# A decoder layer on one core: the inverse root with its own sign, and two of three block sums on GpSimd

## The chip, the core and the metric

The kernel runs on one core of a Trainium2 chip. A core has a matrix engine (TensorE, PE in the profile), a vector engine (VectorE, DVE), a scalar engine (ScalarE, ACT), a general engine (GpSimd, POOL) and SyncE (SP), which issues transfers. They run side by side and wait for each other on semaphores. Operands lie in SBUF, sums of products in PSUM, which has eight banks here. The metric is the device time of one execution in microseconds; lower is better.

## The reference, cut to what matters

One layer of width 1024 on 1024 positions in float32. Every row is normed, multiplied into nine groups of columns, mixed by two kinds of attention, multiplied back and normed again:

```python
def rms_norm(x, g):
    xf = x.astype(jnp.float32)
    y = xf * lax.rsqrt(jnp.mean(xf * xf, axis=-1, keepdims=True) + NORM_EPS)
    return (y * g.astype(jnp.float32)).astype(x.dtype)

def hybrid_layer(x, layer_idx, pre_g, post_g, w_in, ...):
    h = rms_norm(x, pre_g)
    z = jnp.einsum('bsd,de->bse', h, w_in)
    qa, ka, va, ga, qb, kb, vb, gb, gk_low = split_columns(z)
    oa = diff_attention(...)          # 8 heads, softmax minus lam times a second softmax
    oa = rms_norm(oa, subln_g) * (1.0 - lam_init) * silu(ga)
    ob = gla_chunked(...)             # 4 heads, gated linear attention
    ob = rms_norm(ob, gla_g) * silu(gb)
    y = jnp.einsum('bse,ed->bsd', jnp.concatenate([oa, ob], axis=-1), w_out)
    return x + rms_norm(y, post_g)
```

## The kernel before

**Stages.** First x is loaded in eight tiles of 128 rows, normed, transposed and scaled by pre_g: this gives h with the model's columns on the partitions. Then h is multiplied by w_in, pair of column groups after pair, with the results stored to memory (up to about 630 us). Then the scores and weights of the eight softmax heads are made, while PE also multiplies by w_out. At the end eight tiles of y are summed, normed and added to x.

**Products in two parts.** Each float32 operand is cut into a rounded part (hi, a cast on ScalarE) and the rest (lo, a subtraction on DVE), and three products are made of them. `parts` (L545) does it for a block of h, `make_weights` (L278, lines 315 and 316) for a block of w_in, L1096 and L1097 for the weights of the softmax.

**Seven products for eight.** w_in and h are cut into 2 x 2 blocks, and each pair of column groups is multiplied by Winograd's scheme with seven products, numbered 1 to 7 in `order`; `LEFT` says which block or sum of blocks of h each takes: h11, h12, s4, h22, s1, s2, s3. The sums of h's blocks are made in `blocks(j)` for j = 0 to 3, each one quarter of the columns: s1 = h21 + h22 (L565, from PSUM), s3 = h11 - h21 (L568, written over h21) and s2 = s1 - h11 (L569, written over h11, which lies in the tile f1hi). ScalarE and DVE then cut each into hi and lo (L547, L548). s4 = h12 - s2 follows at L625. In the profile the sums' own names are h, f1hi and s. Between two calls of `blocks` PE makes one of the early products (`go(1)`), so that the sums must be ready from product 5 (the tiles named z, which take s1), product 6 (x, which takes s2) and product 7 (s3) on.

**The inverse root.** `rstd` makes 1/sqrt(s + eps) from Ln and Exp on ScalarE and one step of Newton's method on DVE. As it stands, the step ends with (t - 1.5) * r, so its result has the wrong sign. The callers put that right: `scale_x` multiplies by -1 as its second factor, and at the end GpSimd multiplies post_g by -1 (L1408).

**What sets the order.** PE's instructions, and a few that are named in the code (`pin`, `keep_in_program_order`), stand as written. All others are put in order for each engine by a scheduler that has its own times for instructions; it runs when the program is built. Banks of PSUM go round: `take_bank` takes the one that was freed first, so that an early product waits until DVE or ScalarE has read the transposes that had the bank before. DVE's L565 frees such banks.

Of the kernel before, what the change touches and what calls it, by code (L numbers as in the profile page):

```python
# [11 lines left out]
ALU = mybir.AluOpType  # L12
# [19 lines left out]
def hymba_kernel(  # L32
# [20 lines left out]
    nc = tc.nc  # L53
    act, dve, pool, pe, sp = nc.scalar, nc.vector, nc.gpsimd, nc.tensor, nc.sync
# [55 lines left out]
    def take_bank(shape, name):  # L110
        i = free.pop(0)
        return bank(i, shape, name), i
# [6 lines left out]
    def tr(dst, src):  # L119
        tc.keep_in_program_order(pe.transpose(dst, src, ident))  # L120
# [11 lines left out]
    def block(n):  # L132
        if n not in H:
            pool_h, pieces = (hpool, 1) if n in ("s3", "s4") else (hw, 2)
            H[n] = [
                [
                    pool_h.tile(
                        [P, HB // pieces, 512], F32R, tag=f"{n}_{part}{i}", name=f"{n}_{part}"
                    )
                    for i in range(pieces)  # L140
                ]
                for part in ("hi", "lo")
            ]
        return H[n]
# [15 lines left out]
    def t_c(name, dt=F32):  # L160
        return t2k("c", 4, name, dt)
# [317 lines left out]

    def scale_x(st, cs, engine=pool):  # L480
        x_cs = xs[st][:, cs]
        return engine.tensor_scalar(x_cs, x_cs, norms[st], -1.0, ALU.mult, ALU.mult)

    norms, normed = {}, []

    def norm_x(*sts):
        n = len(sts)
        ssq = const.tile([P, 4, n], F32, tag=f"ssq{sts[0]}", name="ssq", bufs=1)
        for i, st in enumerate(sts):
            junk = hw.tile([P, D], F32, tag=("s2_hi0", "s2_lo0")[st % 2], name="junk")  # L490
            ins = act.activation(
                junk, xs[st], AF.Square, scale=D**-0.5, accum_out=ssq[:, 0, i : i + 1]
            )
            if n == 1:
                tc.keep_in_program_order(ins)
        pin = tc.keep_in_program_order if n == 1 else None
        normed[:] = [rstd(nc, ssq[:, :, :n], ssq[:, 0, :n], eps_t, pin)]
        for i, st in enumerate(sts):
            norms[st] = ssq[:, 1, i : i + 1]
            if n == 1:  # L500
                pin(scale_x(st, cols(0), dve))
            else:
                scale_x(st, slice(0, D))
# [12 lines left out]
    for st in range(4):  # L516
        scale_x(st, cols(1))

    def put(ps, k, dst, j):
        hi, lo = dst  # L520
        act.activation(at(hi, j), ps, AF.Copy, scale=pre_g[:, k : k + 1])
        dve.scalar_tensor_tensor(
            at(lo, j), ps, pre_g[:, k : k + 1], fp(at(hi, j)), ALU.mult, ALU.subtract
        )
# [20 lines left out]
    def parts(n, j, f):  # L545
        hi, lo = block(n)
        act.copy(at(hi, j), f)  # L547
        dve.tensor_tensor(at(lo, j), f, fp(at(hi, j)), ALU.subtract)  # L548

    def blocks(j):  # L550


        pss = []
        for k in (j, j + HB):
            ps, i = take_bank([P, 512], "xT")
            for n in range(4):
                tr(ps[:, n * P : (n + 1) * P], xs[4 + n][:, k * P : (k + 1) * P])
            pss.append(ps)
            free.append(i)
        k = j + HB  # L560
        h21 = t_c("h21")
        act.activation(h21, pss[0], AF.Copy, scale=pre_g[:, j : j + 1])
        put(pss[1], k, block("h22"), j)
        s1 = t_c("s1")
        dve.scalar_tensor_tensor(s1, pss[1], pre_g[:, k : k + 1], h21, ALU.mult, ALU.add)  # L565
        parts("s1", j, s1)
        h11 = f1[0][:, j]
        dve.tensor_tensor(h21, h11, h21, ALU.subtract)  # L568
        dve.tensor_tensor(h11, s1, h11, ALU.subtract)  # L569
        parts("s2", j, h11)  # L570
        parts("s3", j, h21)

# [46 lines left out]
    for j in range(HB):  # L619
        blocks(j)  # L620
        go(1)
# [782 lines left out]
    fin = ctx.enter_context(tc.tile_pool(name="fin", bufs=3, reuse_waits="tile"))  # L1404
    post_g = fin.tile([P, D], F32, name="post_g", bufs=1)
    sp.dma_start(post_g, post_norm_g[0:1, :].to_broadcast([P, D]))

    pool.tensor_scalar(post_g, post_g, -1.0, None, ALU.mult)  # L1408
    banks = [Y[0], Y[1], SC[0], SC[1], SC[2], PO, TR[0], TR[1]]
    raws_d, yps, xts = {}, {}, {}  # L1410

# [25 lines left out]
    def finish(n):  # L1437
# [4 lines left out]
        for dh in range(2):  # L1442
# [6 lines left out]
            if not dh:  # L1449
                dve.tensor_scalar(ssq[:, 0], ssq[:, 2], EPS, None, ALU.add)  # L1450
                if n >= NT - LAST:
                    dve.tensor_tensor(y[:, cols(0)], ps_d[st, 0], post_g[:, cols(0)], ALU.mult)
        ins = rstd(nc, ssq, ssq[:, 3], ssq[:, 0])[2]
        if n >= NT - LAST:
            with tc.issue_after(ins.ins):
# [22 lines left out]
def rstd(nc, t, s, eps, pin=None):  # L1478

    pin = pin or (lambda ins: ins)  # L1480
    pin(nc.scalar.activation(t[:, 1], s, AF.Ln, bias=eps))
    exp = pin(nc.scalar.activation(t[:, 1], t[:, 1], AF.Exp, scale=-0.5))
    half = pin(nc.vector.tensor_scalar(t[:, 2], s, eps, 0.5, ALU.add, ALU.mult))
    if t.shape[2] == 1:
        pin(nc.vector.scalar_tensor_tensor(
            t[:, 2], t[:, 1], t[:, 2], t[:, 1], ALU.mult, ALU.mult
        ))
    else:
        pin(nc.vector.tensor_tensor(t[:, 2], t[:, 2], t[:, 1], ALU.mult))
        pin(nc.vector.tensor_tensor(t[:, 2], t[:, 2], t[:, 1], ALU.mult))  # L1490
    last = nc.vector.scalar_tensor_tensor(
        t[:, 1], t[:, 2], 1.5, t[:, 1], ALU.subtract, ALU.mult
    )
    return exp, pin(last), half

# [31 lines left out]
```

## Time and profile before

| | us |
|---|---|
| three runs | 982.34, 983.35, 983.55 (median 983.35) |
| profiled execution | 981.88 |
| its span, first to last instruction | 980.2 |
| busy: PE, DVE, ACT, POOL | 957.5, 737.7, 600.1, 138.1 |
| granted clock of TensorE | 0.998 of full speed |

In the profile a row of a timeline reads: start in us from the span's start, duration in us, engine, line of the kernel, operation, out<-in by the program's names, and in brackets the idle time before it and what ended it. Rows of equal instructions that follow each other are merged (x4). In a list of waits, the engine and line that waited stand first, then what it waited for, the total, how many times, and the longest. PEld is the loading of PE's stationary operand.

### The profile page before, as it was taken

Reading aid. Unit: us, or ns where it says so; the run is one execution under the profiler, and the core shown is the slowest. Engines: PE = TensorE matmul, PEld = TensorE weight load, DVE = VectorE, ACT = ScalarE, POOL = GpSimd, SP = SyncE. Lnnn points to the kernel's source line nnn. Section 1 sums busy time; section 2 is a strip of 40 time slices with the busy share of each in tenths; the row PEclk is TensorE's granted clock in tenths of the full one; section 3 lists DMA queues with packets and bytes.
Section 4 is the critical chain, followed back from the end, with each engine's and each line's share of the span. In section 5 each row is a group of like instructions: output and inputs, shape, how many; then the busy total and the mean of one; then the engine's idle time right before and its main releaser. Section 6 shows DMA issues by size and latency. Waiting matters only on the chain.

```text
span 980.2 us, 15757 instructions
## 1 busy us (share of the span) xinstructions
PE 957.5 (98%) x5338; PEld 829.9 (85%) x5338; DVE 737.7 (75%) x1452; ACT 600.1 (61%) x1164; POOL 138.1 (14%) x143
## 2 busy tenths in 40 slices
PE   6999999999999999999999999999999999999997
PEld 5998988888889998899888888878888888888785
DVE  6986697798866677585885876587888888898555
ACT  8642365486367455445565765366786777787673
POOL 4300000000000010000200100021322222433422
PEclk9999999999999999999999999999999999999999
DMA  9443456747765868896987866997656669994677
GB/s 353 141 122 93 124 153 196 234 164 236 257 228 169 268 193 266 256 292 222 298 255 236 278 208 224 355 308 249 220 173 229 223 208 355 322 288 110 136 210 145
DMA packets 152593, 220.45 MB, mean 225 GB/s; under 512 B 17104, under 2 KB 83664, under 8 KB 152416
## 3 DMA queue, kind: packets, MB, share of 16 engines
q1 hardware_dynamic: 148480, 212.10, 66.8%
q0 software_dynamic: 4032, 7.34, 4.8%
q8 instruction: 42, 0.69, 0.3%
q14 instruction: 39, 0.32, 0.1%
HBM read 133.93 MB, written 88.60 MB: 227 GB/s over the span
## 4 chain that ended last, share of the span: by engine, by line
PE 75%; DVE 8%; DMA 8%; ACT 3%; issue 3%; SPq 1%; POOL 0%; DVEq 0%; ACTq 0%; POOLq 0%
PE x L117 17%; PE ypart L117 12%; PE y L117 12%; PE z L117 12%; PE sc L117 7%; PE po L117 5%; PE yps L117 4%; PE wtr L120 3%; DMA wo_d<-wo_raw 2%; DVE w L316 1%; PE gpo L117 1%; DMA wo_raw<-in_w_out_dram 1%; DVE w_raw L296 1%; DMA w_raw<-in_w_in_dram 1%; DMA mixd<-gate 1%
## 5 line engine op out<-in xcount | busy, mean ns | idle before, releaser
L315 ACT CAST w<-w_raw 128x512 fp32r<-128x512 f32 (+1 forms) x164 | 112.3, 688 | 94.5 <-PE y L117 44.2
L316 DVE TENSOR_TENSOR w<-w_raw,w 128x512 fp32r<-128x512 f32 (+1 forms) x164 | 126.5, 774 | 49.8 <-ACT w L315 43.5
L1048 ACT ACTIVATE p<-p,stt 128x896 f32<-128x896 f32 (+7 forms) x128 | 99.3, 776 | 36.3 <-DVE stt L1038 34.5
L427 ACT COPY s<-x 128x512 f32<-128x512 f32 x84 | 49.1, 584 | 83.2 <-PE x L117 80.2
L296 DVE TENSOR_TENSOR w_raw<-w_raw 128x512 f32<-128x512 f32 (+1 forms) x96 | 76.7, 799 | 15.9 <-DMA w_raw<-in_w_in_dram 14.6
L1054 POOL TENSOR_SCALAR p<-p,stt,lam 128x1024 f32<-128x1024 f32 (+3 forms) x64 | 56.2, 879 | 226.1 <-DVE stt L1053 226.0
L775 POOL TENSOR_SCALAR_AFFINE_SELECT gan<-gan 128x512 f32<-128x512 f32 x8 | 17.3, 2159 | 488.2 <-ACT gan L774 488.2
L1038 DVE CUSTOM_DVE_ANT_0 p<-sc,maskt 128x512 f32<-128x512 f32 (+3 forms) x128 | 74.4, 585 | 15.2 <-PE sc L117 13.7
L117 PE MATMUL z<-s_hi,w 128*128 128x512 f32 x320 | 79.7, 391 | 0.0
L117 PE MATMUL y<-h_hi,w 128*128 128x512 f32 x320 | 79.6, 391 | 0.0
L117 PE MATMUL x<-s_hi,w 128*128 128x512 f32 x320 | 79.6, 391 | 0.0
L117 PE MATMUL ypart<-wo_hi,m_hi 128*128 128x512 f32 x192 | 79.0, 411 | 0.1
L117 PE MATMUL ypart<-wo_hi,m_lo 128*128 128x512 f32 x192 | 75.5, 393 | 0.0
L117 PE MATMUL ypart<-wo_lo,m_hi 128*128 128x512 f32 x192 | 75.4, 393 | 0.0
L117 PE MATMUL sc<-k,q 128*128 128x512 f32 (+1 forms) x192 | 70.5, 371 | 1.5 <-DVE stt L1038 1.5
L117 PEld LDWEIGHTS x<-s_hi,w 128*128 128x128 f32 x320 | 59.7, 188 | 12.2
L117 PEld LDWEIGHTS y<-h_hi,w 128*128 128x128 f32 x320 | 59.6, 188 | 12.2
L117 PEld LDWEIGHTS z<-s_hi,w 128*128 128x128 f32 x320 | 59.5, 188 | 12.0
L117 PE MATMUL sc<-ks,q 128*128 128x512 f32 (+1 forms) x192 | 66.3, 348 | 0.0
L1096 ACT CAST wt_hi<-wtr 128x512 fp32r<-128x512 f32 (+1 forms) x80 | 42.7, 534 | 24.7 <-PE wtr L120 24.3
L1097 DVE TENSOR_TENSOR wt_lo<-wtr,wt_hi 128x512 fp32r<-128x512 f32 (+1 forms) x80 | 50.7, 633 | 7.8 <-ACT wt_hi L1096 7.2
L1057 DVE SCALAR_TENSOR_TENSOR p<-p,stt,p 128x1024 f32<-128x1024 f32 (+3 forms) x64 | 52.1, 814 | 4.7 <-POOL p L1054 4.4
(225 smaller groups left out, 2241.9 us busy)
## 6 DMA issues: line engine op xcount, KB each, us to landing
w_raw<-in_w_in_dram SPq DMA_DIRECT2D x56, 512.0 KB, 4.7
wo_raw<-in_w_out_dram SPq DMA_DIRECT2D x32, 256.0 KB, 3.1
wo_d<-wo_hi SPq DMA_DIRECT2D x32, 256.0 KB, 3.2
wo_d<-wo_raw SPq DMA_DIRECT2D x32, 256.0 KB, 4.2
q<-q_d SPq DMA_DIRECT2D x32, 256.0 KB, 4.7
k<-k_d SPq DMA_DIRECT2D x32, 256.0 KB, 5.5
ks<-k_d SPq DMA_DIRECT2D x64, 128.0 KB, 6.2
wo_hi<-wo_d SPq DMA_DIRECT2D x16, 512.0 KB, 6.4
```

The lines of the kernel that those rows point to most:

```text
L117: tc.keep_in_program_order(pe.matmul(*a, **k))
L120: tc.keep_in_program_order(pe.transpose(dst, src, ident))
L296: dve.tensor_tensor(dst, a, b, ALU.subtract)
L315: act.copy(w[0], src)
L316: dve.tensor_tensor(w[1], src, fp(w[0]), ALU.subtract)
L427: act.copy(b[k], ps)
L1038: ins = dve.tensor_tensor_reduce(p[:, a:e], sc[:, : e - a], maskt[:, NZ + P - (e - a) :] if last else maskt[:, : e - a], 1.0, 3e38 if i == ...
L1048: act.activation(p[:, :n], p[:, :n], AF.Exp, bias=st[:, m : m + 1], scale=-1.0, accum_out=st[:, 2 + m : 3 + m],)
L1054: pool.tensor_scalar(p1[:, :n], p1[:, :n], st[:, 5:6], lam, ALU.mult, ALU.mult)
L1057: dve.scalar_tensor_tensor(p0[:, :n], p0[:, :n], st[:, 4:5], p1[:, :n], ALU.mult, ALU.subtract)
L1096: act.copy(hi[:, :n], pt[:, :n])
L1097: dve.tensor_tensor(lo[:, :n], pt[:, :n], fp(hi[:, :n]), ALU.subtract)
```

## The change

It does three things. The step in `rstd` ends with the right sign: the half takes the factor -0.5 for 0.5 and the last operation adds for it subtracts. So `scale_x` multiplies by 1.0, and the product on post_g on GpSimd is left out. And the two sums L568 and L569 in `blocks`, four times each, are issued on GpSimd and no more on DVE; s1 stays on DVE, since it reads PSUM.

```diff
     def scale_x(st, cs, engine=pool):
         x_cs = xs[st][:, cs]
-        return engine.tensor_scalar(x_cs, x_cs, norms[st], -1.0, ALU.mult, ALU.mult)
+        return engine.tensor_scalar(x_cs, x_cs, norms[st], 1.0, ALU.mult, ALU.mult)
...
         dve.scalar_tensor_tensor(s1, pss[1], pre_g[:, k : k + 1], h21, ALU.mult, ALU.add)
         parts("s1", j, s1)
         h11 = f1[0][:, j]
-        dve.tensor_tensor(h21, h11, h21, ALU.subtract)
-        dve.tensor_tensor(h11, s1, h11, ALU.subtract)
+        pool.tensor_tensor(h21, h11, h21, ALU.subtract)
+        pool.tensor_tensor(h11, s1, h11, ALU.subtract)
         parts("s2", j, h11)
         parts("s3", j, h21)
...
     sp.dma_start(post_g, post_norm_g[0:1, :].to_broadcast([P, D]))
-
-    pool.tensor_scalar(post_g, post_g, -1.0, None, ALU.mult)
...
-    half = pin(nc.vector.tensor_scalar(t[:, 2], s, eps, 0.5, ALU.add, ALU.mult))
+    half = pin(nc.vector.tensor_scalar(t[:, 2], s, eps, -0.5, ALU.add, ALU.mult))
...
     last = nc.vector.scalar_tensor_tensor(
-        t[:, 1], t[:, 2], 1.5, t[:, 1], ALU.subtract, ALU.mult
+        t[:, 1], t[:, 2], 1.5, t[:, 1], ALU.add, ALU.mult
     )
```

The lines up to L1405 keep their numbers; later ones move up by two. The scheduler puts some other instructions in another order too. On DVE, from the s1 of block 1 to the s1 of block 2 (h21_491 and f1hi are block 0's difference and sum, h21_556 block 1's difference, xT_605 block 2's transposes), there stood:

```order
L565 SCALAR_TENSOR_TENSOR s1_560<-xT_551,pre_g_58,h21_556 128x512
L316 TENSOR_TENSOR w_570<-w_early_218,w_570 128x512
L548 TENSOR_TENSOR s2_lo_511<-f1hi_261,s2_hi_509 128x512
L568 TENSOR_TENSOR h21_556<-f1hi_261,h21_556 128x512
L316 TENSOR_TENSOR w_624<-w_early_218,w_624 128x512
L569 TENSOR_TENSOR f1hi_261<-s1_560,f1hi_261 128x512
L548 TENSOR_TENSOR s1_lo_503<-s1_560,s1_hi_501 128x512
L403 TENSOR_TENSOR gv_st_652<-y_627,s_544 128x512
L522 SCALAR_TENSOR_TENSOR h22_lo_496<-xT_605,pre_g_58,h22_hi_494 128x512
L565 SCALAR_TENSOR_TENSOR s1_614<-xT_605,pre_g_58,h21_610 128x512
```

and now stands:

```order
L565 SCALAR_TENSOR_TENSOR s1_560<-xT_551,pre_g_58,h21_556 128x512
L548 TENSOR_TENSOR s3_lo_516<-h21_491,s3_hi_515 128x512
L316 TENSOR_TENSOR w_570<-w_early_218,w_570 128x512
L548 TENSOR_TENSOR s2_lo_511<-f1hi_261,s2_hi_509 128x512
L316 TENSOR_TENSOR w_624<-w_early_218,w_624 128x512
L548 TENSOR_TENSOR s1_lo_503<-s1_560,s1_hi_501 128x512
L403 TENSOR_TENSOR gv_st_652<-y_627,s_544 128x512
L522 SCALAR_TENSOR_TENSOR h22_lo_496<-xT_605,pre_g_58,h22_hi_494 128x512
L565 SCALAR_TENSOR_TENSOR s1_614<-xT_605,pre_g_58,h21_610 128x512
```

The two sums are gone, and the lo part of block 0's difference, which stood ahead of block 1, stands behind its s1. On GpSimd the sums stand between the memsets of a later stage (gkl, wl2), which wait for DVE's second L316 above and for PE's last transposes:

```order
L639 MEMSET ku_773 128x8
L568 TENSOR_TENSOR h21_491<-f1hi_261,h21_491 128x512
L569 TENSOR_TENSOR f1hi_261<-s1_499,f1hi_261 128x512
L568 TENSOR_TENSOR h21_556<-f1hi_261,h21_556 128x512
L569 TENSOR_TENSOR f1hi_261<-s1_560,f1hi_261 128x512
L651 MEMSET gkl_772 128x1024
L646 MEMSET wl2_963 128x768
L568 TENSOR_TENSOR h21_610<-f1hi_261,h21_610 128x512
L569 TENSOR_TENSOR f1hi_261<-s1_614,f1hi_261 128x512
L568 TENSOR_TENSOR h21_666<-f1hi_261,h21_666 128x512
L569 TENSOR_TENSOR f1hi_261<-s1_670,f1hi_261 128x512
```

The memsets stood there before too, with nothing between them. On DVE, ahead of the second L316 of product 6's weights (w_731, the one on which PE waits in the profile) the end of the queue was, from L296 on:

```order
L296 TENSOR_TENSOR w_raw_198<-w_raw_212,w_raw_198 128x1024
L625 TENSOR_TENSOR s4_757<-f1lo_262,f1hi_261 128x512
L569 TENSOR_TENSOR f1hi_261<-s1_670,f1hi_261 128x512
L548 TENSOR_TENSOR s2_lo_512<-f1hi_261,s2_hi_510 128x512
L440 TENSOR_TENSOR c_747<-y_734,s_727 128x512
L548 TENSOR_TENSOR s3_lo_516<-h21_666,s3_hi_515 128x512
L296 TENSOR_TENSOR w_raw_200<-w_raw_200,w_raw_198 128x1024
L316 TENSOR_TENSOR w_731<-w_raw_198,w_730 128x1024
```

In the change the fourth L625 and the last L548 of s2 come ahead of that L316, which they followed; PE's order is the same in both.

## The prediction

> **What bounds the kernel now.** I read the page first, then who waited for whom on TensorE (PE), then the busy times by stretch, and only then the two places where PE waits for VectorE (DVE). The page says that PE is nearly always busy, and GpSimd (POOL) nearly always idle:
>
> ```profile
> span 980.2 us, 15757 instructions
> PE 957.5 (98%) x5338; PEld 829.9 (85%) x5338; DVE 737.7 (75%) x1452; ACT 600.1 (61%) x1164; POOL 138.1 (14%) x143
> ```
>
> So work taken off DVE is worth something only where PE waits for DVE. The waits of PE (what, total us, times, longest) and the busy times of three stretches (length, then PE, PEld, DVE, ACT, POOL, clock, DMA share, GB/s):
>
> ```profile
> PE xT L120 <- DVE x L482: 8.9, 4, 7.4
> PE po L117 <- DVE wt_lo L1097: 1.7, 1, 1.7
> PE y L117 <- DVE s L565: 1.3, 1, 1.3
> ...
> 41.00:60.00 19.00, 17.57 (x124) 16.20 (x122) 19.00 (x29) 9.96 (x16) 0.74 (x1) 1.00 0.17 48
> ...
> 140.00:480.00 340.00, 339.28 (x1967) 300.16 (x1966) 255.28 (x398) 186.94 (x321) 13.09 (x6) 1.00 0.72 231
> 480.00:920.00 440.00, 438.02 (x2249) 369.77 (x2248) 341.22 (x809) 301.12 (x624) 90.21 (x94) 1.00 0.78 249
> ```
>
> From 41 to 60 us, where the sums of h's blocks are made, DVE is busy for 19.00 of 19.00 us while PE stands still for 1.4 us: PE has almost no cover left there. From 140 to 920 us PE is idle for 0.72 + 1.98 us, so a delay that it takes at 60 us finds next to nothing to absorb it and arrives at the end nearly whole. The clock is 1.00 in all three. The 8.9 us at L482 are the first loads and norms; the change gives them another factor of the same cost and no other order.
>
> **Part 1: eight sums go from DVE to GpSimd.** L568 and L569 run four times each. What DVE is spared is read from this timeline (start, us, engine):
>
> ```profile
> 32.91 1.03 PE L120 MATMUL xT<-ident,xt 128*128 128x128 f32 x8
> ...
> 36.77 0.68 DVE L316 TENSOR_TENSOR w<-w_early,w 128x512 fp32r<-128x512 f32 x1
> ...
> 39.45 1.12 PE L117 MATMUL y<-w,h_lo 128*128 128x256 f32 x8
> ...
> 40.61 0.69 DVE L403 TENSOR_TENSOR gv_st<-y,s 128x512 f32<-128x512 f32 x1
> 41.22 0.74 DVE L522 SCALAR_TENSOR_TENSOR h_lo<-xT,pre_g,h_hi 128x512 fp32r<-128x512 f32 x1
> 41.87 0.74 DVE L565 SCALAR_TENSOR_TENSOR s<-xT,pre_g,h 128x512 f32<-128x512 f32 x1
> 42.76 2.14 PE L117 MATMUL y<-w,h_hi 128*128 128x256 f32 x16 [1.32 <-DVE s L565]
> ...
> 49.19 0.69 DVE L569 TENSOR_TENSOR f1hi<-s,f1hi 128x512 f32<-128x512 f32 x1
> 49.79 0.69 DVE L568 TENSOR_TENSOR h<-f1hi,h 128x512 f32<-128x512 f32 x1
> 50.39 0.69 DVE L548 TENSOR_TENSOR s_lo<-h,s_hi 128x512 fp32r<-128x512 f32 x1
> 51.60 1.22 DVE L296 TENSOR_TENSOR w_raw<-w_raw 128x1024 f32<-128x1024 f32 x1
> 53.08 1.12 PE L117 MATMUL z<-w,s_lo 128*128 128x256 f32 x8
> 56.87 1.22 DVE L316 TENSOR_TENSOR w<-w_raw,w 128x1024 fp32r<-128x1024 f32 x1
> 56.92 2.44 PE L117 MATMUL x<-w,s_hi 128*128 128x256 f32 x16
> ```
>
> Starts of neighbours are 0.60 us apart (49.19, 49.79, 50.39), so each sum moved frees 0.60 us of DVE. Of its other instructions in the walk below, those with 512 columns take 0.60 (L522 and L565 0.65, by 41.22 and 41.87), those with 1024 1.15. What they cost on GpSimd, and what this does to DVE, is shown a little earlier, where GpSimd makes four two-input sums of the same shape (L542) while DVE has other work; the last row is the group of the four (count, then busy us and mean ns):
>
> ```profile
> 18.16 1.28 POOL L542 TENSOR_TENSOR f1hi<-h_hi,h_lo 128x512 f32<-128x512 f32 x1
> 19.41 2.27 POOL L542 TENSOR_TENSOR f1hi<-h_hi,h_lo 128x512 f32<-128x512 f32 x1
> ...
> 18.18 2.34 DVE L296 TENSOR_TENSOR w_raw<-w_raw 128x1024 f32<-128x1024 f32 x1
> 20.45 1.25 DVE L1483 TENSOR_SCALAR ssq<-ssq,eps_t 128x2 f32<-128x2 f32 x1
> 21.69 1.21 DVE L296 TENSOR_TENSOR w_raw<-w_raw 128x1024 f32<-128x1024 f32 x1
> ...
> L542 POOL TENSOR_TENSOR f1hi<-h_hi,h_lo 128x512 f32<-128x512 f32 x4 | 6.0, 1529 | 3.0 <-DVE h_lo L522 3.0
> ```
>
> Read them as turns. The GpSimd sum that starts at 18.16 runs its 1.28 us; the DVE subtraction issued at 18.18 takes 2.34 us instead of 1.21, because it begins when that sum ends (18.16 + 1.28 = 19.44, and 19.44 + 1.1 = 20.5). The next GpSimd sum, 2.27 us instead of 1.28, begins when the DVE instruction ends, and a DVE instruction on two columns waits 1.25 us for it. The two engines take turns, instruction by instruction, and whoever waited longest goes next. DVE instructions that read PSUM are outside of it: during GpSimd's L482, four instructions from 23.93 to 29.34, this one took the usual 0.74 us:
>
> ```profile
> 23.93 5.41 POOL L482 TENSOR_SCALAR xt<-xt,ssq 128x1024 f32<-128x1024 f32 x4 [2.25 <-ACT h_hi L521]
> 25.16 0.74 DVE L522 SCALAR_TENSOR_TENSOR h_lo<-xT,pre_g,h_hi 128x512 fp32r<-128x512 f32 x1
> ```
>
> Of DVE's instructions around the sums, L548, L316, L296 and L625 read two operands from SBUF, so these can be held; L522, L565, L403 and L440 read PSUM. The unknown is for how long each new GpSimd sum holds DVE: at least 0, at most 1.53 us (the mean of the four L542, their own waits included); I take 1.25, the spacing of two starts (18.16 to 19.41).
>
> Now the queue. By the order of the changed program, DVE goes from block 1's L565 to the L316 on which PE waits last (started at 56.87) as follows. I let a GpSimd sum go once its L565 is done and DVE's current instruction has ended. Block 1: s_lo 36.7 to 37.3, GpSimd's L568 to 38.5, L316 to 39.1, L569 to 40.4, s_lo, L316, s_lo to 42.2, then L403, L522, L565 from 43.4. This L565 freed PE's bank from 41.87 before: PE restarts 1.5 us late. Block 2, whose first GpSimd sum follows the two memsets: s_lo to 44.7, L568 to 45.9, L625 to 46.5, L569 to 47.8, L625, s_lo, L522, L565, s_lo to 50.9. Block 3: L568 to 52.1, s_lo to 52.7, L569 to 54.0, L316 to 55.1, L625, L403, three s_lo and one more to 58.1 (PE wants the last s_lo of s1 soon after its 53.08), L296, L625, s_lo, L440, L296 to 62.2. The L316 then starts at 62.2 against 56.87, 5.3 us late, and PE's second third of that x with it.
>
> The same from the other side: in the 20.1 us from 36.77 to 56.87 six of the eight sums leave (6 x 0.60 = 3.6; block 0's two lie ahead of it, where DVE waits for block 1's transposes, which PE starts at 32.91, anyway); by the new order three instructions of 0.60 us come to stand ahead of the L316 (a first s_lo, the last L625 and the last s_lo: +1.8); six holds of 1.25 come in, each of them with an L548, L316 or L625 next on DVE (+7.5). -3.6 + 1.8 + 7.5 = +5.7, less the idle moments that it fills. I take the walk's **+5.3 us**. From there DVE and PE are late together, and no further wait arises: ScalarE has half of its time free in that stretch (9.96 of 19.00). Its casts of s2 and s3 now wait for GpSimd, with bank-freeing L562 and weight cast L315 queued behind them, but in the walk they come ahead of the DVE instruction that uses them.
>
> The GPSIMD Engine Reference of the Trainium skill, section Elementwise — side-by-side cycle accounting, measures 4497 ns for such a sum on 2048 columns; a quarter is, as an estimate, 1.12 us. By that the sum would be 6 x 0.13 us smaller, +4.5; the row with the duration decides.
>
> **Part 2: the product on post_g goes (L1408).** Here are the last DVE wait of PE and what lies around it:
>
> ```profile
> 925.56 2.69 DVE L1348 TENSOR_TENSOR m_lo<-m_raw,m_hi 128x384 fp32r<-128x384 f32 x2
> 925.99 3.12 POOL L1408 TENSOR_SCALAR post_g<-post_g 128x1024 f32<-128x1024 f32 x1
> 926.36 0.62 ACT L1129 CAST sq_hl<-sq 64x512 fp32r<-64x512 f32 x1
> 927.41 0.50 PE L117 MATMUL po<-wt_hi,v 128*128 128x256 f32 x2
> 928.28 0.69 DVE L1130 TENSOR_TENSOR sq_hl<-sq,sq_hl 64x512 fp32r<-64x512 f32 x1
> 929.00 0.56 DVE L1097 TENSOR_TENSOR wt_lo<-wtr,wt_hi 128x384 fp32r<-128x384 f32 x1
> 929.61 0.39 PE L117 MATMUL po<-wt_lo,v 128*128 128x256 f32 x1 [1.70 <-DVE wt_lo L1097]
> ...
> 946.79 0.56 DVE L1232 TENSOR_TENSOR m_lo<-m_raw,m_hi 128x384 fp32r<-128x384 f32 x1
> ```
>
> Two DVE instructions take 2.69 us; one of that shape takes 0.56 (946.79). Without the hold they end near 926.7; L1130 waits for ACT until 926.98 and ends at 927.6; L1097 starts at 927.62 instead of 929.00. That is **-1.4 us**, with bounds of 0 (L1408 is not what holds) and -1.7 (PE's whole wait). The chain that ended last shows why it arrives whole; from 930.56 on it is PE alone (with one ms product between):
>
> ```profile
> 930.56 8.41 PE yps L117 x37
> ...
> 939.20 34.28 PE yps L117 x151
> ```
>
>  That ScalarE's order in the last tiles changes (the seeds of tile 4 ahead of an Exp) costs nothing: some five instructions of 0.6 us now stand ahead of tile 4's operands, while PE spends 24 matmuls of 34.28 / 151 = 0.23 us, 5.4 us, on the tile before.
>
> **Other edits.** The signs in rstd and scale_x are other constants in the same instructions: 0. In the first scores one L1057 moves ahead of a 0.48 us score instruction; PE waits earlier but for the same next bank: 0, at most 0.5 either way.
>
> Sum: +5.3 - 1.4 = **+3.9 us**. The profiled execution took 981.88 us with a span of 980.2, 1.5 under the median of 983.35; a span of 984.1 is expected and, added to the median, 987.2 us.
>
> **Rivals.** (a) *No turns*: these forms run side by side, as the undisturbed 1.28 of the sum at 18.16 might suggest. Then DVE is free early; but L403 still waits for PE's y, which ends at 40.57 (39.45 + 1.12), L565 still starts near 41.8, and only the wait for L316 (0.3 us: the x of 16 takes 2.44, the y of the same shape 2.14) and 0.3 more are won: -0.6 - 1.4 = -2.0, 981.3. Against it: 2.34 beside 1.21. (b) *DVE keeps its turn*: a DVE instruction that stands ready goes before GpSimd's, whose sums start only where DVE idles or reads PSUM. Then some 0.6 us of each hold lies under such an instruction: 5.3 - 6 x 0.6 - 1.4 = +0.3, 983.7. Against it: at 20.45 DVE had an instruction ready, and GpSimd went. The SBUF — State Buffer page of the Trainium skill, section Who interferes with whom, has it that issue order decides who is blocked, not the kind of instruction; this would come out as (b) where DVE always issues first. (c) *L1408 did not hold DVE*, since a descriptor-writing L1313 stands right before it: no gain in part 2, +5.3, 988.6. (d) *Longer holds*, 1.53 each: 1.7 more, 988.9.
>
> **How the numbers follow.** Forecast 0.60 (986 to 988.3), (a) 0.12, (b) 0.13, (c) 0.08, (d) 0.07. About 0.2%, 2 us, is what a measurement here can tell from no change. Slower by more: forecast, (c), (d), less some 0.05 of the forecast that falls short: 0.70. Within: (b) and that rest, 0.17. Faster: (a) at its edge, 0.13. The range goes from 981.8, short of (a), to 989.0, beyond (d).
>
> **What would show it.** Right: DVE rows L548, L316, L625 of 1.9 to 2.4 us between 37 and 55 us; eight POOL rows of 1.3 to 1.9; PE's y at 44.2 and the next z's and x's with a DVE wait, together 5 to 7 us between 41 and 65; L1348 back at 0.55 and the 1.70 us wait below 0.5. Wrong: DVE rows of 0.69 beside the GpSimd sums (then (a)), or GpSimd sums of 2 us and more with DVE undisturbed (then (b)).

## The result and the profile after

The changed kernel is slower by half a per cent. It was timed twice, on two occasions, each time beside the kernel before:

| | median us | executions | kernel before, median us | ratio, 95% interval |
|---|---|---|---|---|
| first | 990.13 | 5 | 983.35 | 1.0052 (1.0034 to 1.0070) |
| again (below) | 987.27 | 6 | 983.62 | 1.0046 (1.0031 to 1.0061) |

The forecast of 987.2 us is a ratio of 1.0039, which lies in both intervals. Its range ended at 989.0: the first median is above it, the second inside. The profiled execution is one of the first five (990.13 us), the span first:

```profile
span 988.4 us, 15753 instructions
```

The span is 8.2 us longer. Who waited for whom on PE (total us, times, longest):

```profile
PE y L117 <- ACT s L427: 2.2, 1, 2.2
PE y L117 <- DVE s L565: 2.1, 1, 2.1
PE x L117 <- DVE w L316: 1.5, 1, 1.5
...
PE z L117 <- DVE w L316: 0.8, 1, 0.8
```

The last three are what the walk of the prediction was about. The first was not foreseen: before the change it was 0.68 us. The turns themselves, from the timeline of GpSimd and DVE (start, us, engine):

```profile
36.80 1.60 POOL L568 TENSOR_TENSOR h<-f1hi,h 128x512 f32<-128x512 f32 x1 [0.81 <-ACT s_hi L547]
38.48 1.63 POOL L569 TENSOR_TENSOR f1hi<-s,f1hi 128x512 f32<-128x512 f32 x1
41.32 0.95 POOL L651 MEMSET gkl<- 128x1024 f32 x1 [1.21 <-DVE w L316]
...
37.18 1.78 DVE L316 TENSOR_TENSOR w<-w_early,w 128x512 fp32r<-128x512 f32 x1
38.88 1.78 DVE L548 TENSOR_TENSOR s_lo<-f1hi,s_hi 128x512 fp32r<-128x512 f32 x1
41.18 0.68 DVE L548 TENSOR_TENSOR s_lo<-s,s_hi 128x512 fp32r<-128x512 f32 x1
...
44.30 3.48 DVE L625 TENSOR_TENSOR s<-f1lo,f1hi 128x512 f32<-128x512 f32 x2
50.23 1.77 DVE L548 TENSOR_TENSOR s_lo<-h,s_hi 128x512 fp32r<-128x512 f32 x1
51.93 2.31 DVE L316 TENSOR_TENSOR w<-w_raw,w 128x1024 fp32r<-128x1024 f32 x1
61.24 1.21 DVE L316 TENSOR_TENSOR w<-w_raw,w 128x1024 fp32r<-128x1024 f32 x1
```

Six DVE instructions are held, each beside one GpSimd sum: four rows here, and the merged row of the two L625. A row of 512 columns takes 1.78 us when held and 0.68 when not, so a hold costs 1.10 us. GpSimd pays too: 1.6 us for a sum that takes 1.28 undisturbed. DVE's rows follow each other without idle time from 36 to 67 us in this trace, so DVE never stood waiting for a result of GpSimd there. The memset at 41.32, which reads nothing, leaves the L548 at 41.18 alone. The SBUF — State Buffer page of the Trainium skill, section Who interferes with whom, has just this: a DVE instruction with two SBUF inputs contends with a GpSimd instruction that reads SBUF, and not with one that only writes. The trace agrees.

Here are two of the waits that follow from it, and then the one that was not foreseen, step by step over ScalarE, DVE, SP and PE:

```profile
43.92 2.14 PE L117 MATMUL y<-w,h_hi 128*128 128x256 f32 x16 [2.13 <-DVE s L565]
...
62.50 1.21 PE L117 MATMUL x<-w,s_hi 128*128 128x256 f32 x8 [1.47 <-DVE w L316]
...
59.61 2.18 ACT L547 CAST s_hi<-s 128x512 fp32r<-128x512 f32 x4
61.70 0.62 ACT L362 ACTIVATE qk_hi<-c 128x512 fp32r<-128x512 f32 x1
...
62.37 2.48 DVE L548 TENSOR_TENSOR s_lo<-s,s_hi 128x512 fp32r<-128x512 f32 x4
64.78 0.68 DVE L363 SCALAR_TENSOR_TENSOR c<-c,qk_hi 128x512 fp32r<-128x512 f32 x1
...
62.35 1.14 SPq L367 DMA_DIRECT2D k_d<-qk_hi  x2
63.59 1.36 SPq L194 DMA_DIRECT2D w_raw<-in_w_in_dram  x1
65.49 1.08 SPq L367 DMA_DIRECT2D k_d<-c  x2
66.66 1.65 SPq L194 DMA_DIRECT2D w_raw<-in_w_in_dram  x2
...
72.65 1.23 DVE L296 TENSOR_TENSOR w_raw<-w_raw 128x1024 f32<-128x1024 f32 x1 [4.74 <-DMA w_raw<-in_w_in_dram]
73.96 1.04 ACT L315 CAST w<-w_raw 128x1024 fp32r<-128x1024 f32 x1 [5.78 <-DVE w_raw L296]
74.91 0.58 ACT L427 COPY s<-x 128x512 f32<-128x512 f32 x1
75.54 2.64 PE L117 MATMUL y<-w,h_hi 128*128 128x256 f32 x16 [2.24 <-ACT s L427]
```

Read it backwards. PE waits for the copy L427, which stands on ScalarE behind the cast L315. That cast waits for DVE's L296, and L296 for the load of w_raw issued at 66.66. This load stands on SP behind an earlier load (63.59) and behind two stores: that of qk_hi, which the cast L362 makes, and that of c, which DVE's L363 makes. L362 stands behind the four casts of s4, and L363 behind the four L548 of s4. Before the change both stood ahead of them, and the two loads were issued at 58.12 and 61.11, 5.5 us earlier, while PE is 4.35 us late by then:

```profile
55.26 0.63 ACT L362 ACTIVATE qk_hi<-c 128x512 fp32r<-128x512 f32 x1 [0.58 <-DVE c L440]
...
58.12 0.39 SPq L194 DMA_DIRECT2D w_raw<-in_w_in_dram  x1
61.11 3.91 SPq L194 DMA_DIRECT2D w_raw<-in_w_in_dram  x2
...
64.92 1.23 DVE L296 TENSOR_TENSOR w_raw<-w_raw 128x1024 f32<-128x1024 f32 x1 [0.34 <-DMA w_raw<-in_w_in_dram]
```

The second load also takes longer to land: 6.0 us from its issue to the L296 that waits for it (66.66 to 72.65), against 3.8 before (61.11 to 64.92). Now it follows closely on the first load and the stores, all on one queue; that this is why it takes longer was not shown.

What PE did after that pause, in stretches of 2 us (length, PE busy, granted clock, DMA share, GB/s):

```profile
74.00:76.00 2.00, 0.46 (x3) 1.00 0.01 1
76.00:78.00 2.00, 2.00 (x16) 0.75 0.37 131
78.00:80.00 2.00, 2.00 (x11) 0.50 0.38 132
80.00:82.00 2.00, 2.00 (x17) 0.90 0.00 0
```

The clock falls to half for about 3.4 us: (0.25 + 0.50 + 0.10) x 2 us = 1.7 us of PE's work is lost. After the pause of 2.13 us that ends at 43.92, nearly as long, it does not fall; the last section shows why.

Matching PE's instructions of the two traces one by one gives the account of the 8.2 us: 0.34 at the start (26 us), 4.35 at the x of 62.50, 5.91 at the y of 75.54, 7.39 when the clock is back, 9.42 at 879 us, 8.26 at 938. So 4.0 us come from the holds (less what DVE was spared), 1.56 from the late load, 1.48 from the clock and 2.0 from what lies between 81 and 879 us. At the end 1.16 come back. Of the 2.0 us, 0.5 come back before 640 us, and 2.5 are lost in short waits in the stage of the scores behind it. These differ from execution to execution: between 640 and 880 us the other profiles below lose 0.0 to 3.2 us against the kernel before, among them 0.4 and 2.2 in two kernels that have the sign part and no sums on GpSimd. They are not put down to the change.

The tail is as forecast: L1348 (two in one row) takes half a us each, and PE's wait for L1097 is 0.43 where it was 1.70.

```profile
935.09 1.02 DVE L1348 TENSOR_TENSOR m_lo<-m_raw,m_hi 128x384 fp32r<-128x384 f32 x2
937.87 0.39 PE L117 MATMUL po<-wt_lo,v 128*128 128x256 f32 x1 [0.43 <-DVE wt_lo L1097]
```

### The profile page after: what moved, and what is told of

Read it like the earlier page. It is cut to its first block, busy times and chain, and to the rows that moved or that the text cites. A ratio compares the mean times of both kernels' runs of the same rounds, so it can differ in the third digit from the quotient of the medians.

```text
span 988.4 us, 15753 instructions
## 1 busy us (share of the span) xinstructions
PE 960.4 (97%) x5338; PEld 832.2 (84%) x5338; DVE 739.7 (75%) x1444; ACT 601.6 (61%) x1164; POOL 146.6 (15%) x150
## 4 chain that ended last, share of the span: by engine, by line
PE 82%; DVE 7%; DMA 5%; ACT 3%; SPq 1%; issue 1%; DVEq 0%; ACTq 0%
PE x L117 20%; PE z L117 14%; PE y L117 14%; PE ypart L117 11%; PE sc L117 6%; PE po L117 5%; PE yps L117 4%; PE wtr L120 3%; PE gpo L117 2%; DMA ks<-k_d 1%; DVE w L316 1%; PE kv L117 1%; DVE s_lo L548 1%; DMA wo_raw<-in_w_out_dram 1%; PE gkl_ps L117 1%
## 5 line engine op out<-in xcount | busy, mean ns | idle before, releaser
L315 ACT CAST w<-w_raw 128x512 fp32r<-128x512 f32 (+1 forms) x164 | 112.4, 688 | 101.8 <-PE y L117 46.4
L316 DVE TENSOR_TENSOR w<-w_raw,w 128x512 fp32r<-128x512 f32 (+1 forms) x164 | 127.6, 780 | 53.1 <-ACT w L315 44.7
L427 ACT COPY s<-x 128x512 f32<-128x512 f32 x84 | 49.2, 585 | 84.0 <-PE x L117 83.8
L296 DVE TENSOR_TENSOR w_raw<-w_raw 128x512 f32<-128x512 f32 (+1 forms) x96 | 75.9, 791 | 17.0 <-DMA w_raw<-in_w_in_dram 15.6
L1097 DVE TENSOR_TENSOR wt_lo<-wtr,wt_hi 128x512 fp32r<-128x512 f32 (+1 forms) x80 | 50.6, 632 | 7.5 <-ACT wt_hi L1096 7.1
```

Source lines behind the costliest of these rows:

```text
L296: dve.tensor_tensor(dst, a, b, ALU.subtract)
L315: act.copy(w[0], src)
L316: dve.tensor_tensor(w[1], src, fp(w[0]), ALU.subtract)
L427: act.copy(b[k], ps)
L1097: dve.tensor_tensor(lo[:, :n], pt[:, :n], fp(hi[:, :n]), ALU.subtract)
```

## The experiments

Each ratio is to the kernel before on the same chip: medians 984.47 us (first four), 983.62 (next four), 983.53 (last two).

### The two parts apart

The sign part alone (the sums stay `dve.tensor_tensor`):

> Only the sign part of the change: rstd ends with its own sign, scale_x multiplies by 1.0, no product on post_g; all sums of h's blocks stay on DVE. Part 2 of the prediction: DVE's two L348-type instructions behind it take 0.55 us each again, PE's wait for L1097 near 922 us falls from 1.70 to about 0.4, the time falls by 1.3 us to 982.0 (981.6 to 982.8). Rival (the product never held DVE): no change, 983.3, with the 1.70 us wait still there.

Measured: 981.86 us, 0.9982 (0.9970 to 0.9994). In its profile PE's wait for L1097 is 0.43 us:

```profile
928.94 0.38 PE L117 MATMUL po<-wt_lo,v 128*128 128x256 f32 x1 [0.43 <-DVE wt_lo L1097]
```

So the product did hold DVE, and its removal is a gain of its own.

The sums part alone (the sign and its product as before):

> Only the sums part: L568 and L569 on GpSimd, the sign as before with its product on post_g. If the parts add up: the changed kernel's 990.1 plus 1.3, so 991.4 (990.5 to 992.5), with the six DVE rows of 1.8 to 2.3 us between 37 and 55 us and the 1.70 us wait for L1097 back. Rival (the sign part moves the order of the first tiles and carries some of the loss): 988 or less.

Measured: 990.26 us, 1.0063 (1.0046 to 1.0079), a little under the 990.5 to 992.5 expected. Six held rows, and the product holds DVE again:

```profile
933.21 2.69 DVE L1348 TENSOR_TENSOR m_lo<-m_raw,m_hi 128x384 fp32r<-128x384 f32 x2
937.25 0.39 PE L117 MATMUL po<-wt_lo,v 128*128 128x256 f32 x1 [1.70 <-DVE wt_lo L1097]
```

By ratio the parts are -1.8 and +6.2 us, together +4.4, against +4.5 to +5.1 for the whole: they add up within their intervals.

### Holds without anybody waiting for GpSimd

```diff
-        h11 = f1[0][:, j]
+        h11, h12 = f1[0][:, j], f1[1][:, j]
+        for op in (ALU.add, ALU.subtract): pool.tensor_tensor(h12, h12, s1, op)
         dve.tensor_tensor(h21, h11, h21, ALU.subtract)
```

> The kernel before, with eight sums of 128x512 added on GpSimd that nothing needs in time: after each s1 GpSimd adds s1 to f1lo and subtracts it again (the result differs by rounding only). DVE keeps all its own sums; the order on every other engine is the one before. Theory of turns: between 36 and 53 us some six DVE instructions on two SBUF operands take 1.1 us longer, DVE has no idle time there to lose, so the L316 of w_731 starts 5 to 7 us after 56.87 and the time is 989 to 991. Theory that the loss comes from waiting for GpSimd's results, or from the new order: 983.4, DVE rows at 0.69.

Measured: 990.10 us, 1.0063 (1.0047 to 1.0078). From DVE and PE (the line of s1 is L564 here):

```profile
42.31 1.75 DVE L568 TENSOR_TENSOR h<-f1hi,h 128x512 f32<-128x512 f32 x1
64.52 1.21 DVE L316 TENSOR_TENSOR w<-w_raw,w 128x1024 fp32r<-128x1024 f32 x1
47.94 3.58 PE L117 MATMUL y<-w,h_hi 128*128 128x256 f32 x16 [5.05 <-DVE s L564]
```

The order on DVE, ScalarE, SP and PE is that of the kernel before, and yet the L316 of w_731 starts at 64.52 and not at 56.87. 1.4 us of this were there before the first added sum (the s1 of block 0 started at 33.20 and not at 31.78), the other 6.2 came after it. DVE makes its own sums in the same order, and what is new there is the held rows. A loss of this size can thus be made by GpSimd's reading alone, with DVE doing all its own work and nobody waiting for GpSimd's results. That the ratio is the same as that of the sums part, 1.0063, is chance: here DVE keeps its own sums, PE stands still for 5.05 us at once, and the clock fell in all six executions; there the sums leave DVE and the late load comes in. The rival that PE waits for GpSimd's results falls by this and by DVE's unbroken work in the changed kernel.

### Two instructions put back

The changed kernel, with the casts and subtractions of s4 sent behind L362 and L363:

```diff
-            act.activation(hi, c, AF.Copy, scale=scale)
-            dve.scalar_tensor_tensor(lo, c, scale, fp(hi), ALU.mult, ALU.subtract)
+            cut[0] = act.activation(hi, c, AF.Copy, scale=scale)
+            cut[1] = dve.scalar_tensor_tensor(lo, c, scale, fp(hi), ALU.mult, ALU.subtract)
...
-    for j in range(HB):
-        parts("s4", j, s4[j // 2][:, j % 2])
+    with tc.issue_after(cut[0].ins), tc.issue_after(cut[1].ins):
+        [parts("s4", j, s4[j // 2][:, j % 2]) for j in range(HB)]
```

> The changed kernel, with two instructions put back where they stood before the change: ScalarE's L362 ahead of the four casts of s4, DVE's L363 ahead of the four subtractions of s4. Nothing else moves on any engine. Theory: in the changed kernel SP's loads of w_raw stand behind the store of L362's and L363's results, so they start at 63.6 and 66.7 us; here they start at about 62.2 and 64.2, the L296 that waits for them starts near 70.3 instead of 72.65, PE's wait for ScalarE's L427 near 74 us falls from 2.24 to about 0.7 us, and without that pause the clock stays at 1.00 from 76 to 82 us: 990.1 - 1.5 - 1.5 = 987.1 (986.3 to 988.0). If the pause goes but the clock falls all the same: 988.6. Rival (the loads are late because their buffers come free late, 4.4 us of holds): no change, 990.1.

Measured: 986.13 us, 1.0021 (1.0010 to 1.0031). From SP, DVE and PE:

```profile
60.47 1.14 SPq L367 DMA_DIRECT2D k_d<-qk_hi  x2
62.08 0.39 SPq L194 DMA_DIRECT2D w_raw<-in_w_in_dram  x1
66.22 1.71 SPq L194 DMA_DIRECT2D w_raw<-in_w_in_dram  x2
...
69.79 1.23 DVE L296 TENSOR_TENSOR w_raw<-w_raw 128x1024 f32<-128x1024 f32 x1 [2.27 <-DMA w_raw<-in_w_in_dram]
73.60 2.18 PE L117 MATMUL y<-w,h_hi 128*128 128x256 f32 x16 [0.68 <-ACT s L427]
```

The first load leaves 1.5 us earlier. The others hardly move, against the expectation (66.22, not 64.2): in this trace the second load waits 2.4 us on SP for DVE's L316, which frees its buffer, so that the rival of the late buffers is right for its issue. Yet L296 gets its data at 69.79, 3.6 us after the issue and not 6.0, and the 2.24 us pause is 0.68 again. So of the 2.9 us that L296 gains 0.4 come from an earlier issue and 2.5 from a shorter landing. By the times, two moved instructions carry 2.5 to 3 of the 4.5 to 5.1 us of the changed kernel (1.0046 and 1.0052 less 1.0021, each difference with about 2 us of uncertainty). In this execution the clock fell after the pause at 42 us, the very pause after which it had stayed up in the changed kernel:

```profile
46.00:48.00 2.00, 2.00 (x11) 0.50 0.00 0
```

There it costs little: PE runs into its next waits for DVE and arrives at the x of product 6 with the same 4.0 us.

### Work taken out of DVE's queue ahead of that L316

The kernel of the last experiment, and s4's subtractions sent behind w_731's L316 (`lows[i]` is the L316 of product i):

```diff
-    for j in range(HB):
-        dve.tensor_tensor(s4[j // 2][:, j % 2], f1[1][:, j], f1[0][:, j], ALU.subtract)
+    with tc.issue_after(lows[order.index((0, 6))].ins):
+        [dve.tensor_tensor(s4[j // 2][:, j % 2], f1[1][:, j], f1[0][:, j], ALU.subtract) for j in range(HB)]
```

> The changed kernel with L362 and L363 in their old places (ratio 1.0021), and the four subtractions L625 (s4, not needed before about 80 us) sent behind the L316 of w_731 on DVE, with some neighbours changing places. Theory that DVE's queue up to that L316 is what sets PE's time there, held instructions and all: four times 0.60 us leave the queue, the L316 starts about 2 us earlier, PE's waits between 41 and 63 us shrink by about 2 us in sum, ratio 1.000 (0.999 to 1.001). The holds stay: six DVE rows of 1.8 to 2.3 us, now on other instructions. Rival (PE waits for GpSimd's sums themselves, through the casts of s2 and s3): no change, 1.0021.

Measured: 985.38 us, 1.0018 (1.0006 to 1.0030). DVE's rows:

```profile
43.97 1.77 DVE L548 TENSOR_TENSOR s_lo<-f1hi,s_hi 128x512 fp32r<-128x512 f32 x1
...
57.40 1.21 DVE L316 TENSOR_TENSOR w<-w_raw,w 128x1024 fp32r<-128x1024 f32 x1
```

In the trace it does what was expected: the holds go over to other instructions, the L316 starts at 57.40 (60.84 without the edit), PE's only DVE wait of 0.5 us or more between 36 and 70 us is the 2.1 us for L565, and PE is 2.0 us earlier at that x. In time hardly any of it is seen: the interval holds the rival's 1.0021, and of the theory's 0.999 to 1.001 only the upper edge. The clock had fallen here too, after the pause at 42 us; with DVE no longer the bound behind it, what it costs (1.5 us in this trace) now reaches the end. 5 of the 12 executions have a clock of 0.997 or less. So the trace supports the theory, and the time leans to the rival and does not confirm the gain.

### How often the clock falls

The changed kernel once more:

> The changed kernel itself once more, beside the others on this chip, for more executions of it. With all that was seen so far: ratio to the kernel before 1.0055 (1.004 to 1.007); PE's 2.24 us pause near 74 us in the profile, and a granted clock below 0.998 in about half of the executions (2 of 5 so far), because that pause and the 2.1 us one at 42 us are sometimes followed by a few us at half clock. If the clock has nothing to do with the pauses: 0.998 or 0.999 in nearly all, as in the kernel with the sign part alone.

Measured: 987.27 us, 1.0046 (1.0031 to 1.0061); one of six executions below 0.998, fewer than expected. In the profiled one PE's wait for L427 was 1.42 us, and not the 2.24 expected, since the load landed earlier, and the clock stayed up. So the late load cost 1.56 us and a fall of the clock in one profiled execution of the changed kernel, and 0.74 us in the other.

The pause made without GpSimd, on the kernel with the sign part alone (four copies, or two, in place of one):

```diff
-            act.copy(b[k], ps)
+            for _ in range(4 if (p, n) == (0, 7) else 1): act.copy(b[k], ps)
```

> The kernel with the sign part alone (981.9 us, clock 0.998 or 0.999 in all of 12 executions), in which ScalarE makes one copy (L427, on which PE waits near 69.6 us) four times in place of once: PE's pause there grows from 0.68 to about 2.2 us, as long as the one of the changed kernel near 74 us, with nothing on GpSimd. Some DVE instructions behind it change places. Theory that a pause of that length can bring the clock down: 1.6 us more from the pause in all executions, and in a part of them a clock of 0.996 or 0.997 and up to 2 us more: 983.5 to 985, with half clock in the profile behind 71 us if it falls in that execution. Rival (the clock falls for another reason): 983.5, clock 0.998 or 0.999 in all.

> The same with two copies in place of one: PE's pause there is about 1.2 us. Theory: 0.5 us more, 982.4, and the clock stays at 0.998 or 0.999 in all executions, since pauses of 1.3 us at 42 us leave it there in the kernel with the sign part alone. If short pauses count too: clocks of 0.997 and less, and 983 or more.

Measured: 984.85 us, 1.0013 (1.0005 to 1.0022), four of twelve executions below 0.998; and 981.94 us, 0.9980 (0.9968 to 0.9993), none of twelve. The profiled execution of the long pause is one in which the clock did not fall, after 2.53 us:

```profile
72.35 2.18 PE L117 MATMUL y<-w,h_hi 128*128 128x256 f32 x16 [2.53 <-ACT s L427]
```

So a pause of this length can bring the clock down but need not. In the times themselves the four executions with the lower clock (984.36 to 985.49) are not apart from the other eight (983.08 to 985.77): what a single fall costs is read from the traces, not from these medians.

### A version that beats both

The sign part, the late L625, and on DVE L403 behind the L565 of its block:

```diff
...
-            dve.tensor_tensor(st, p0, p1, ALU.add)
+            with tc.issue_after(s1s[-1].ins) if s1s else nullcontext():
+                dve.tensor_tensor(st, p0, p1, ALU.add)
...
```

> A version that takes the reading of the stretch at its word: the sign part, all sums on DVE, the four L625 behind the L316 of w_731, and on DVE the bank-freeing L565 of a block ahead of L403 (gv_st), which it followed. Theory (DVE's order and load up to 60 us set PE's waits): the L565 of block 2 ends 0.7 us earlier, PE's wait of 1.3 us there becomes 0.6, the 0.3 us wait for w_731 goes, and nothing comes in their place: 1.0 us less than with the sign part alone (ratio 0.9981), so 0.9971 (0.996 to 0.9985). Rival: PE waits as long as before at the next DVE result, since DVE's whole work up to there is the same: 0.998.

> The same without the change of place of L565 and L403: the sign part, all sums on DVE, the four L625 behind the L316 of w_731. PE's 1.3 us wait for L565 stays, since that lies ahead; only the 0.3 us wait for w_731 goes: ratio 0.9978 (0.9965 to 0.999). In the kernel with the sums on GpSimd the same edit took 1.9 us out of PE's waits, since there PE waited 1.5 us for that L316.

Measured: 981.13 us, 0.9979 (0.9967 to 0.9991), and without the L403 edit 981.60 us, 0.9983 (0.9972 to 0.9994). In the first (its lines from L404 on are one higher), PE's wait for L565 is down from 1.32 to 0.49 us:

```profile
42.57 2.14 PE L117 MATMUL y<-w,h_hi 128*128 128x256 f32 x16 [0.49 <-DVE s L566]
```

Counted from 26 us, where this execution is 0.55 us behind the one with the sign part alone, PE is 0.7 us ahead of it at 60 us, not 1.0: something did come in place of the old waits, since the late L625 delay the last s_lo of the x and PE waits 0.23 us for it. At 660 us a wait of 1.5 us for a load (ks<-k_d) eats the gain in the profiled execution. All three versions beat the kernel before by about 0.2%, and none can be told from the sign part alone (0.9982). That is the change to keep.

## Why the prediction came out as it did

**The turns** (part 1, first half) were right in kind and place. Each of the six holds lies on the instruction that the walk gave it, PE's y restarts at 43.92 (forecast 44.2), and DVE rows around the GpSimd sums are 1.77 to 2.31 us. The term was mis-sized: a hold is 1.10 us, not the 1.25 taken from two starts of GpSimd, and one turn of each engine takes 1.70 us (37.18 to 38.88), less than GpSimd's 1.28 and DVE's 0.60 together. The L316 of w_731 starts 4.0 us late (61.24 - 0.34 - 56.87), not 5.3. Six times 0.15 is 0.9 of the 1.3. The rest is mostly that block 0's two sums did free some time, against the working: block 1's L565 starts at 35.92 - 0.34 = 35.58 us, 0.5 earlier than the 36.11 before. (In the walk of block 3, "three s_lo and one more" names one too many; its times count three.) The estimate from the GPSIMD Engine Reference of the Trainium skill, section Elementwise — side-by-side cycle accounting (1.12 us for a sum, +4.5 in all), came nearer than the spacing of two starts, by luck: the sum whose duration it estimates takes 1.28 us undisturbed, and a hold is shorter than that. PE's waits for DVE between 41 and 65 us are 2.1 + 0.8 + 0.5 + 1.5 = 4.9 us, just short of the 5 to 7 forecast.

**"From there DVE and PE are late together, and no further wait arises"** is the step that failed. The working followed ScalarE for the casts of s2 and s3 and left out L362 and DVE's L363, which the scheduler had moved behind the casts and subtractions of s4, and SP's queue, in which the loads of the next weights stand behind the stores that these two feed. The profiled execution paid 1.56 us for the pause and 1.48 for the clock behind it, the other profiled one 0.74 and nothing; the experiment that puts the two instructions back is 2.5 to 3 us faster, with about 2 us of uncertainty. The hold term was too large by 1.3 us and this term was missing. That the sum came out nearer than its parts is luck.

**Part 2** was right: forecast -1.4, PE's wait fell by 1.27, and the kernel with this part alone is 1.8 us faster (0.6 to 3.0). That the clock falls less often without this pause may carry the rest of it; this was not shown in the times.

**The rivals.** *No turns* and *DVE keeps its turn* fall by the six rows of 1.77 to 2.31 us. *L1408 did not hold DVE* falls by the sign part alone. *Longer holds* fall by 1.10. The 0 for the other edits stands: nothing at scale_x, the first scores or the last tiles shows in any comparison, though the scatter of up to 3 us in the score stage would hide a few tenths.

## What to carry to other kernels

Moving an elementwise operation with two SBUF inputs to GpSimd is no relief for a VectorE whose own next instruction also reads two SBUF operands: here each of eight sums freed 0.60 us and six of them cost 1.10 each; look first at what VectorE will run beside it. When a scheduler sorts the program anew, compare the order on every queue, and follow each moved instruction to the stores it feeds and to the loads behind those stores. Where a kernel is bound by TensorE, a pause of 2 us in it can cost some 1.5 us more in clock, as it did here in some executions.

## What the hardware showed that was not expected

How often the granted clock of an execution was 0.997 or less. 0.998 is what the end of the program alone leaves, where PE has no work (0.57 and 0.50 in the last two stretches of 2 us of the profile before). The second column is the longest wait of PE after the first 30 us in the profiled execution; other executions of the same kernel can have other waits (the 1.9 and the 1.5 lie in the later stages, which the edits do not touch).

| kernel | longest wait, us | clock 0.997 or less |
|---|---|---|
| sign part alone; with two copies; with L403 behind L565 | 1.3; 1.3; 1.5 | 0 of 36 |
| kernel before | 1.7 | 38 of 75 |
| sign part, late L625 | 1.9 | 2 of 12 |
| L362 and L363 put back | 2.1 | 2 of 12 |
| the same, late L625 | 2.1 | 5 of 12 |
| changed kernel, both times | 2.2; 2.1 | 3 of 11 |
| four copies | 2.5 | 4 of 12 |
| sums part alone | 2.1 and 1.7 | 5 of 6 |
| added sums | 5.0 and 1.7 | 6 of 6 |

In kernels whose longest wait was 1.5 us the clock never fell; in those with 1.7 us and more it did so sometimes, and the same pause did so in one execution and not in the next. The traces show what decides. In all twelve the clock changes only at multiples of 3.413 us, counted from its first rise (18.98 us in the changed kernel's first profile), and a fall lasts one such window. Here are four windows of that profile, two over the pause that ends at 43.92 and two from the one that ends at 75.54 (length, PE busy, granted clock, DMA share, GB/s):

```profile
39.46:42.87 3.41, 2.33 (x21) 1.00 0.00 0
42.87:46.28 3.41, 2.36 (x20) 1.00 0.22 77
73.59:77.00 3.41, 1.46 (x12) 1.00 0.02 3
77.00:80.41 3.41, 3.41 (x18) 0.50 0.44 154
```

The first pause is cut in two by a border: PE stands still for 1.08 us of one window and 1.05 of the next, and the clock stays up. Of the second, 1.95 us lie in one window, and the next window runs at half clock. In the twelve traces a fall in the middle of the kernel follows each of the six windows in which PE stood still for 1.78 us or more, and none of those with 1.50 or less. The 2.53 us pause of the four copies was cut into 1.03 and 1.50. In the sums part alone the clock fell after the 1.70 us wait for L1097, which lay whole in one window, with 0.08 us of short gaps beside it.

The falls in the traces cost 1.4 to 1.6 us of PE's time each. The Trainium skill's page TensorE: Matmul & The Clock Gate, Part 1, tells of windows of 3413 ns that run free of the program; the traces agree. By the same page the clock falls after an idle window, about 3.4 us; here 1.8 us of idle time within one window were enough, and the measurement decides. If the borders lie at random, the 1.70 us pause of the kernel before lies whole in one window in (3.41 - 1.70) / 3.41 = half of the executions, as an estimate, and 38 of 75 were counted. For the 2.53 us of the four copies, of which at least 1.78 must lie in one window, the same estimate is (3.41 - 1.78 + 2.53 - 1.78) / 3.41 = 0.70, and 4 of 12 were counted: why so few is open.
